# A down product with six of eleven row pairs in seven block products, and a copy moved ahead of rounding in one gate tile

## The chip, the cores and the metric

The kernel runs on 1 core of a Trainium2 chip. The metric is the device time of one execution in microseconds (us). Five engines work side by side and meet by semaphores: PE (TensorE, matmuls), DVE (VectorE), ACT (ScalarE), POOL (GpSimd) and SP (SyncE, which issues most DMAs). Each engine takes its instructions in the order of the program.

## The reference

One decoder layer over S = 512 positions of width D = 1024, in float32: a combined input projection, four retention heads, four attention heads over keys that an indexer selects, an output projection, a layer norm, and then a SwiGLU feed-forward of 2816 hidden columns with a last layer norm. Only the feed-forward's part matters here:

```python
FFN_HIDDEN = -(-(8 * D_MODEL) // (3 * 256)) * 256      # 2816
# x (512, 1024) after the first norm; wgu (1024, 2 x 2816), wd (2816, 1024)
gate, up = split(x @ wgu)
h = silu(gate) * up                                    # (512, 2816)
y = layer_norm(DEEPNORM_ALPHA * x + h @ wd, lfg, lfb)  # (512, 1024)
```

The layer norm takes mean and variance over the 1024 columns of a position, then gain `lfg` and bias `lfb`.

## The kernel before

**Precision.** Every product is made of three matmuls in a rounded float32 type (`mm3`, lines 94 to 96): high x high, high x low and low x high halves of the two operands. A helper `split` makes the halves: ACT casts to the high half (L86); the low half is either a subtraction on DVE (L91), or, where the engine is given as None, ACT copies the negated high source (L88, scale -1) and a DMA that POOL issues adds to it in place (L89, an accumulate).

**Staging.** The hidden width is cut into 22 tiles of 128 rows. The gate and up products run over 22 cycles `g_cycle(n)`, each of which already multiplies by blocks: sums of weight blocks (`g_sum`, on DVE) are split (`g_conv(n, kind)`, kinds A to D) and multiplied with sums of activation blocks, 128x256 a matmul (`g_mm`, L846); copies from PSUM (`t7` is the copy on L907, followed by the add on L916) and an order written out by hand tie the cycles together. In cycle n the splits of tile n+1 and n+2 are made. The results are the hidden activations `hu`, tiles [128 hidden, 512 positions], four to a buffer.

**Down product.** The 22 hidden tiles make 11 pairs. The output's 1024 columns are done in two halves of 512: first the left half for all pairs (banks `left`, in the profile `dl`), then the right (`right`, in the profile `dr`). For a pair m, `conv_w` splits 1024 weight columns a partition (`dh`, `dl` as weight tiles, from `draw`, a ring of three raw buffers that SP loads), `conv_h` splits the two hidden tiles once (`h`), and `d_mm` multiplies into the four position blocks b, two hidden tiles by three matmuls of 128x512 each. Weight halves lie in rings of four (`wh`, `wl`), so a cast for step i+4 waits for PE to leave step i. `take` adds a bank to the residual `y` (ALPHA y + bank), `stat` collects the norm's statistics. The last four pairs of the right half go block by block, so that each block's norm runs under the next block's matmuls; the last block's right half ends in a bank of its own (`dc`). The norm's gain and bias are loaded into `gf` (`gbf`) at the start of the stage.

The schedule is manual: each engine's order is the order of the code.

Of the kernel before, what the change touches and what calls it, by code (L numbers as in the profile page):

```python
# [15 lines left out]
P = 128  # L16
# [37 lines left out]
def hybrid_layer_kernel(ctx: ExitStack, tc: tile.TileContext, xT, x, pos, w0, wf, wt, wo,  # L54
# [12 lines left out]
    def psd(name):  # L67
        return psp.tile([P, 512], F32, tag="d", name=name)
# [987 lines left out]
    def d_load(j):
        c, g = divmod(j, 6)
        if c < 2:
            draw[j] = wp.tile([P, 4, S], F32, tag="raw", name=f"draw{j}")
            for k in range(2 * g, min(2 * g + 2, HC)):  # L1060
                i = 2 * (k % 2)
                dma(draw[j][:, i:i + 2], wd[k, :, :, c * S:c * S + S])

    def conv_w(i):
        if i >= 2 * HC:
            return
        c, m = divmod(i, HC)
        j = 6 * c + m // 2
        wh = wp.tile([P, 1024], F32R, tag="wh", bufs=4, name=f"dh{i}")
        wl = wp.tile([P, 1024], F32R, tag="wl", bufs=4, name=f"dl{i}")  # L1070
        src = draw[j][:, 2 * (m % 2):2 * (m % 2) + 2].rearrange("p k c -> p (k c)")
        split(V, wh, wl, src)
        dw[i] = wh, wl
        if m % 2 or m == HC - 1:
            d_load(j + 3)

    def conv_h(m):
        if m >= HC:
            return
# [12 lines left out]
        for k in range(2):  # L1092
            dh[2 * m + k] = hi[:, k * S:k * S + S], lo[:, k * S:k * S + S]

    def d_mm(acc, i, b, first, last, cs=slice(0, S)):
        wh, wl = dw[i]
        for k in range(2):
            h, l = dh[2 * (i % HC) + k]
            bs = slice(b * P, b * P + P)
            ws = slice(k * S + cs.start, k * S + cs.stop)  # L1100
            mm3(acc, h[:, bs], l[:, bs], wh[:, ws], wl[:, ws], first and k == 0, last and k == 1,
                **({} if cs.start == 0 and cs.stop == S else {"skip_group_check": True}))

    y = x1
    cl, cr = slice(0, S), slice(S, D)
# [49 lines left out]
    conv_w(2)  # L1155
    conv_h(2)
    for b in range(3):
        for i in range(2):
            d_mm(left[b], i, b, i == 0, False)
    conv_w(3)  # L1160
    conv_h(3)
    for i in range(2):
        d_mm(left[3], i, 3, i == 0, False)
    for i in range(2, HC):
        conv_w(i + 2)
        conv_h(i + 2)
        for b in range(NB):
            d_mm(left[b], i, b, False, i == HC - 1)

    right = [psd(f"dr{b}") for b in range(NB)]  # L1170
    for i in range(HC, 2 * HC - TAIL):
        conv_w(i + 2)
        if i - HC < NB:
            take(i - HC, cl, left[i - HC])
            stat(i - HC, 0, cl)
        for b in range(NB):
            d_mm(right[b], i, b, i == HC, b == NB - 1 and i == 2 * HC - TAIL - 1)
# [100 lines left out]
```

## Time and profile before

| | us |
|---|---|
| median of 3 runs (628.85 to 629.33) | 629.03 |
| the profiled execution's own time | 628.54 |
| its span in the profile | 626.8 |
| PE busy (3768 matmuls) | 617.3 |
| DVE busy | 478.2 |
| ACT busy | 299.6 |
| POOL busy | 95.4 |

The times of instructions in the trace count from the start of the span. The span is a little shorter than the execution's own time, which also holds what lies around it. An engine's busy time is the union of its instructions, without the issuing of DMAs; matmuls are pipelined, so that one lasts longer than the distance to the next. "x2" in a row of the timeline joins two instructions of one kind that follow each other. A releaser in brackets is what ended the idle time before an instruction.

### The profile page before, as it was taken

How to read it: one execution, taken by the hardware profiler on the slowest of the kernel's cores; microseconds unless marked ns; L12 is line 12 of the kernel's file. 1: busy time of each engine (PE TensorE's matmuls, PEld its weight loads, DVE VectorE, ACT ScalarE, POOL GpSimd, SP SyncE). 2: the span in 40 equal slices, each digit the busy share in tenths (PEclk: the TensorE clock that was granted, in tenths of full speed). 3: DMA queues.
4: the chain of work that ended last, by engine and by line, in shares of the span. 5: the costliest groups of instructions: out<-in, count | busy, mean ns of one | idle time of the engine just before them, and what ended most of it. 6: DMA issues, size and time to landing. Idle time of an engine off the chain costs nothing.

```text
span 626.8 us, 9712 instructions
## 1 busy us (share of the span) xinstructions
PE 617.3 (98%) x3768; PEld 551.8 (88%) x3768; DVE 478.2 (76%) x893; ACT 299.6 (48%) x529; POOL 95.4 (15%) x101
## 2 busy tenths in 40 slices
PE   9999999999999999999999999999999999999995
PEld 7988888888888778889999999999999988888884
DVE  6798687898879877899989898988889764333256
ACT  5644445335334656877555465555555653212200
POOL 1176322421463000332000000000000000000011
PEclk9999999999999999999999999999999999999999
DMA  9877344888534952894431323233231461422002
GB/s 316 280 225 222 108 122 110 213 170 196 136 104 138 339 217 68 207 179 102 151 135 68 135 73 131 84 119 115 89 135 68 151 220 67 135 90 79 0 35 100
DMA packets 25885, 88.24 MB, mean 141 GB/s; under 512 B 2752, under 2 KB 6144, under 8 KB 20208
## 3 DMA queue, kind: packets, MB, share of 16 engines
q1 hardware_dynamic: 18624, 71.51, 32.7%
q0 software_dynamic: 6480, 14.88, 12.7%
q10 hardware_dynamic: 736, 1.25, 0.6%
q8 instruction: 29, 0.48, 0.3%
q14 instruction: 16, 0.13, 0.1%
HBM read 69.80 MB, written 2.10 MB: 115 GB/s over the span
## 4 chain that ended last, share of the span: by engine, by line
PE 84%; DVE 9%; issue 3%; POOL 1%; ACT 1%; POOLq 0%; DVEq 0%; ACTq 0%
PE ga L846 17%; PE gc L846 9%; PE pf L95 5%; PE pf L94 5%; PE pf L96 5%; PE gb L846 4%; PE acc L205 4%; PE dl L94 3%; PE dl L96 3%; PE dl L95 3%; PE dr L96 3%; PE dr L94 3%; PE dr L95 3%; PE pt L94 2%; PE pt L96 2%
## 5 line engine op out<-in xcount | busy, mean ns | idle before, releaser
L91 DVE TENSOR_TENSOR dl<-draw,dh 128x1024 fp32r<-128x1024 f32 x22 | 26.9, 1225 | 59.0 <-ACT dh L86 59.0
L435 POOL TENSOR_TENSOR rs<-ve,half 128x1 f32<-128x1 f32 (+1 forms) x11 | 11.8, 1069 | 382.0 <-DVE ve L434 381.8
L86 ACT CAST wh<-raw 128x1024 fp32r<-128x1024 f32 x44 | 45.9, 1049 | 47.1 <-issue 19.8
L86 ACT CAST dh<-draw 128x1024 fp32r<-128x1024 f32 x22 | 23.1, 1049 | 68.1 <-PE dl L96 37.1
L94 PE MATMUL pf<-xh,wh 128*128 128x512 f32 x128 | 50.0, 391 | 0.0
L95 PE MATMUL pf<-xl,wh 128*128 128x512 f32 x128 | 50.0, 390 | 0.0
L96 PE MATMUL pf<-xh,wl 128*128 128x512 f32 x128 | 49.9, 390 | 0.0
L91 DVE TENSOR_TENSOR wl<-raw,wh 128x1024 fp32r<-128x1024 f32 x25 | 30.6, 1234 | 17.8 <-ACT wh L86 17.4
L94 PE MATMUL pt<-wh,xh 128*128 128x512 f32 x96 | 39.1, 408 | 0.0
L96 PE MATMUL pt<-wh,xl 128*128 128x512 f32 x96 | 37.5, 391 | 0.0
L95 PE MATMUL pt<-wl,xh 128*128 128x512 f32 x96 | 37.4, 390 | 0.0
L94 PE MATMUL dl<-dh,h 128*128 128x512 f32 x88 | 34.2, 389 | 0.0
L95 PE MATMUL dl<-dl,h 128*128 128x512 f32 x88 | 34.2, 389 | 0.0
L96 PE MATMUL dl<-dh,h 128*128 128x512 f32 x88 | 34.2, 389 | 0.0
L96 PE MATMUL dr<-dh,h 128*128 128x512 f32 (+1 forms) x88 | 33.4, 379 | 0.0
L95 PE MATMUL dr<-dl,h 128*128 128x512 f32 (+1 forms) x88 | 33.4, 379 | 0.0
L94 PE MATMUL dr<-dh,h 128*128 128x512 f32 (+1 forms) x88 | 33.4, 379 | 0.0
L815 DVE TENSOR_TENSOR gs<-graw,gs 128x512 f32<-128x512 f32 x44 | 30.3, 689 | 0.8
L815 DVE TENSOR_TENSOR gs<-graw 128x512 f32<-128x512 f32 x44 | 30.1, 685 | 0.0
L96 PEld LDWEIGHTS pf<-xh,wl 128*128 128x128 f32 x128 | 24.0, 188 | 5.2
L94 PEld LDWEIGHTS pf<-xh,wh 128*128 128x128 f32 x128 | 24.0, 188 | 4.6
L95 PEld LDWEIGHTS pf<-xl,wh 128*128 128x128 f32 x128 | 24.1, 188 | 4.6
(974 smaller groups left out, 1911.2 us busy)
## 6 DMA issues: line engine op xcount, KB each, us to landing
graw<-in_wgu_dram SPq DMA_DIRECT2D x22, 1024.0 KB, 4.8
draw<-in_wd_dram SPq DMA_DIRECT2D x22, 512.0 KB, 3.9
wl<-raw POOLq DMA_DIRECT2D x19, 512.0 KB, 5.8
raw<-in_wf_dram SPq DMA_DIRECT2D x8, 1024.0 KB, 6.7
raw<-in_wo_dram SPq DMA_DIRECT2D x8, 1024.0 KB, 4.9
raw<-in_wt_dram SPq DMA_DIRECT2D x6, 1024.0 KB, 5.1
w0s<-in_w_dram SPq DMA_DIRECT2D x8, 320.0 KB, 5.0
x<-in_x_dram SPq DMA_DIRECT2D x4, 512.0 KB, 5.7
```

What stands on the lines that cost most here:

```text
L86: A.copy(hi, src)
L91: eng_lo.tensor_tensor(lo, src, hi.bitcast(F32), op=ALU.subtract)
L94: T.matmul(acc, lhsT=lh, rhs=rh, start=first, stop=False, **kw)
L95: T.matmul(acc, lhsT=lh, rhs=rl, start=False, stop=False, **kw)
L96: T.matmul(acc, lhsT=ll, rhs=rh, start=False, stop=last, **kw)
L205: T.matmul(acc0[i][:, o:], lhsT=a[:, i * P:i * P + P], rhs=b[kt][:, o:], start=(kt == 0 and p == 0), stop=(kt == KT - 1 and p == 2))
L435: G.tensor_tensor(r[:, :n], e[:, :n], half[:, :n], op=ALU.pow)
L815: eng.tensor_tensor(t[dst], a, b, op=ALU.subtract)
L846: T.matmul(gp[n][acc], lhsT=a[:, i * S + k * P:i * S + k * P + P], rhs=parts[q][:, b, k], start=first and j == 0, stop=j == 11, skip_group ...
```

## The change

**Gate tile 2.** In the cycle of tile 2 the split of kind A for tile 3 stands behind the copy `t7` and its add, no longer ahead of them.

**Down product.** The pairs 0, 1, 2, 3 and 10 stay plain. The pairs 4 to 9 make three units (2, 3, 4) of two pairs. In a unit the positions are cut into two halves of 256, the hidden rows by pairs of tiles and the output columns into the left and right 512, and the 2x2 block product is made of seven products (q = 1 to 7) of sums of blocks in place of eight. Each product of a unit is one step: `w_prep(i)` splits its weights (step i+4 is prepared behind step i), `aprep` its activations, and `w_mm(i)` makes 12 matmuls of 128x512 into two banks. The order is q = 1, 5, 6, 2, 7, 4, 3, for each q the units 2, 3, 4. The banks X, Y and `left` gather products of several q and are added to `y` by `take` and by the new uses of `add_to`. New on DVE are the sums of blocks (s1 to s4 of activations, in the tiles `ts` and `t3s`; t1, t2, t4 of weights in the tiles `tw` or in place, t3 in place). Where `low` is None (the weights of q = 1, the activations of q = 1, 2, 7, 4, 3) the low halves go through POOL's accumulate: 3 of 512 KB and 15 of 256 KB; the down stage before had none. A sum or a product is named with its unit behind it: t1_2 is t1 of unit 2, p7_3 the split weights of q = 7 of unit 3, r1_4 the raw weights r1 of unit 4. Raw weights come as r1, r2a, r2b, r3a, r4, r5a, r5b through the same ring of three buffers. The gain and bias `gbf` are loaded in the middle of the stage (behind step 10), no longer at its start. The tail by blocks takes the plain pairs 0 to 3 and uses `add_to`.

```diff
         if n == 1:
             for m in range(FIRST):
                 g_silu1(m)
-        else:
+        if n not in (1, 2):
             g_conv(n + 1, "A")
...
         V.tensor_tensor(gp[n]["t7"], gp[n]["t7"], c, op=ALU.add)
+        if n == 2:
+            g_conv(3, "A")
...
+    PLAIN = [0, 1, 2, 3, 10]
+    UNITS = [2, 3, 4]
...
+    def wprep(key, pieces, low=V):
+        wh = wp.tile([P, 1024], F32R, tag="wh", bufs=4, name=f"dh{key}")
+        wl = wp.tile([P, 1024], F32R, tag="wl", bufs=4, name=f"dl{key}")
+        n = 1024 // len(pieces)
+        for i, src in enumerate(pieces):
+            hi, lo = (t[:, i * n:i * n + n] for t in (wh, wl))
+            if len(src.shape) == 3:
+                hi, lo = (t.rearrange("p (k c) -> p k c", c=S) for t in (hi, lo))
+            split(low, hi, lo, src)
+        dw[key] = wh, wl
...
+    def aprep(q, j, src, low):
+        i, half = divmod(slot_n[0], 2)
+        if half == 0:
+            slot_n[1] = big.tile([P, 2, 2, S], F32R, tag=slot_tags[i], name=f"slot{i}")
+        slot_n[0] += 1
+        t = slot_n[1][:, half]
+        split(low, pq(t[:, 0]), pq(t[:, 1]), src)
+        da[q, j] = t
...
+    def s1_(j):
+        ts[j] = tmp(f"ts{j}")
+        V.tensor_tensor(pq(ts[j]), blk(j, 1, 0), blk(j, 1, 1), op=ALU.add)
+
+    def s2_(j):
+        V.tensor_tensor(pq(ts[j]), pq(ts[j]), blk(j, 0, 0), op=ALU.subtract)
...
+    def t2_(j):
+        for q in range(2):
+            V.tensor_tensor(b22(j)[:, q], b22(j)[:, q], tw[j, q], op=ALU.subtract)
+
+    def t4_(j):
+        for q in range(2):
+            V.tensor_tensor(tw[j, q], b21(j)[:, q], b22(j)[:, q], op=ALU.subtract)
...
+    WORDER = [(q, j) for q in (1, 5, 6, 2, 7, 4, 3) for j in UNITS]
+
+    def w_prep(i):
+        q, j = WORDER[i]
+        prep[q](j)
...
+    def w_mm(i, banks, first):
+        q, j = WORDER[i]
+        wh, wl = dw[f"p{q}_{j}"]
+        a = da[q, j]
+        for n in range(2):
+            for t in range(2):
+                ss = slice(n * Q + t * P, n * Q + t * P + P)
+                ws = slice(n * S, n * S + S)
+                mm3(banks[t], a[:, 0, ss], a[:, 1, ss], wh[:, ws], wl[:, ws], first and j == UNITS[0] and n == 0,
+                    j == UNITS[-1] and n == 1, skip_group_check=True)
...
-    gf = big.tile([P, 2, D], F32, tag="s4", name="gbf")
-    for i, v in enumerate((lfg, lfb)):
-        dma(gf[:, i], row(v, D))
...
+    for j in UNITS:
+        s1_(j)
+    for j in UNITS:
+        aprep(1, j, blk(j, 0, 0), None)
+    conv_h(10)
+    t1_(2)
+    conv_w(0, 10)
+    r1_load(4)
+    w_prep(0)
+    r2a = raw_load("r2a", [(i, wd[4 + i, :, 1, S:]) for i in range(4)])
...
+    l_step(3)
+    for j in UNITS:
+        s2_(j)
+    for j in UNITS:
+        aprep(6, j, pq(ts[j]), V)
+    t2_(2)
+    w_prep(2)
+    r3a = raw_load("r3a", [(i, wd[4 + i, :, 1, :S]) for i in range(4)])
+    t2_(3)
+    t2_(4)
...
+    home_of = {1: X, 5: Y, 6: X, 2: left[:2], 7: X, 4: left[2:]}
+    gf = None
+    for i in range(18):
+        q, j = WORDER[i]
+        w_mm(i, home_of[q], q in (1, 5))
...
+        elif i == 7:
+            aprep(7, 2, pq(t3s[2]), None)
+            t3_(2)
+        elif i == 8:
+            for u in (3, 4):
+                aprep(7, u, pq(t3s[u]), None)
+        elif i == 9:
+            t3_(3)
+        elif i == 10:
+            t3_(4)
+            for u in UNITS:
+                aprep(4, u, blk(u, 1, 1), None)
+            gf = big.tile([P, 2, D], F32, tag="s8", name="gbf")
+            for k, v in enumerate((lfg, lfb)):
+                dma(gf[:, k], row(v, D))
+        elif i == 12:
+            for u in UNITS:
+                aprep(3, u, pq(ts[u]), None)
...
+        if i < 17:
+            w_prep(i + 4)
...
+        if i == 3:
+            r4_load(2)
+        elif i == 7:
+            r4_load(3)
+            r4_load(4)
+        elif i == 8:
+            r5a = raw_load("r5a", [(n, wd[4 + n, :, 1, S:]) for n in range(4)])
+        elif i == 9:
+            r5b = raw_load("r5b", [(n, wd[8 + n, :, 1, S:]) for n in range(2)] + [(2, wd[10, :, :, S:])])
+        elif i == 10:
+            d_load(1, 0)
+        elif i == 15:
+            d_load(1, 1)
...
+    for i in range(18, 21):
+        w_mm(i, [right[0], right[1]], True)
+        conv_w(1, last4[i - 18])
+    for b in (2, 3, 0, 1):
+        d_mm(right[b], 1, 10, b, b >= 2, True)
+    conv_w(1, last4[3])
```

On ACT in the cycle of gate tile 2 (`gt` are `t2` and `t7`, `ga` and `gc` banks of PSUM, `gh3A` the high half of the split of kind A for tile 3, `gs` its sums), the difference reads:

```order
 L86 CAST gh2D<-graw_2579 128x512
 L885 COPY gt_2985<-ga_2692 128x256
+L907 COPY gt_2985<-ga_2692 128x256
 L86 CAST gh3A<-gs_1_2946 128x512
 L86 CAST gh3A<-gs_0_2945 128x512
-L907 COPY gt_2985<-ga_2692 128x256
 L86 CAST gh4B<-graw_2857 128x512 x2
```

The copy has moved ahead of the two casts; on DVE the add that reads it has moved ahead of gl3A's two subtractions in the same way.

On ACT in the first part of the down stage (`draw` and `r` are raw weights, `hu` the hidden activations), the order before was:

```order
-L86 CAST dh_5506<-draw_5401 128x1024
-L86 CAST h_1_5510<-hu_3109 128x1024
-L86 CAST dh_5550<-draw_5401 128x1024
-L86 CAST h_1_5510<-hu_3109 128x1024
-L86 CAST dh_5571<-draw_5492 128x1024
-L86 CAST h_2_5575<-hu_3630 128x1024
```

and what stands some way behind the same first four rows now (`slot` holds split activations, `ts` their sums, `dhp_4_...` and `dlp_4_...` the halves of p1_4, the weights of q = 1 of unit 4; `r_4_5595` is r1_4):

```order
+L86 CAST dhp_3_5643<-r_3_5550 128x1024
+L88 ACTIVATE dlp_3_5644<-r_3_5550 128x1024
+L86 CAST slot_5684<-ts_5567 128x512
+L86 CAST slot_5684<-ts_5569 128x512
+L86 CAST slot_5689<-ts_5571 128x512
+L86 CAST dhp_4_5694<-r_4_5595 128x1024
+L88 ACTIVATE dlp_4_5695<-r_4_5595 128x1024
```

Casts of weights and of activations took turns one pair at a time; now the weights of q = 1 of unit 4 stand behind the three casts of the sums for q = 6, and their low half is a copy on ACT that an accumulate of POOL follows.

On ACT in the middle of the block steps (`dhp_2_5938`, `dhp_3_5962` and `dhp_4_5996` are the weights of q = 7 for units 2, 3 and 4, from r4; `slot<-hu` are activations of q = 4):

```order
+L86 CAST dhp_2_5938<-r_2_5832 128x1024
+L86 CAST dhp_3_5962<-r_3_5913 128x1024
+L86 CAST slot_5934<-hu_3630 128x512
+L88 ACTIVATE slot_5934<-hu_3630 128x512
+L86 CAST slot_5986<-hu_4151 128x512
+L88 ACTIVATE slot_5986<-hu_4151 128x512
+L86 CAST slot_5986<-hu_4672 128x512
+L88 ACTIVATE slot_5986<-hu_4672 128x512
+L86 CAST dhp_4_5996<-r_4_5916 128x1024
```

Where before one cast of 1024 weight columns followed another, six operations of 512 columns now stand between the weights of units 3 and 4. On SP the loads that feed this place, with what follows them, are now (`r_2_5832`, `r_3_5913` and `r_4_5916` are r4 of units 2, 3 and 4):

```order
+L80 DMA r2b<-in_wd_dram 128x512 x4
+L80 DMA r3a<-in_wd_dram 128x512 x4
+L80 DMA r_2_5832<-in_wd_dram 128x2x512 x2
+L80 DMA r_3_5913<-in_wd_dram 128x2x512 x2
+L80 DMA r_4_5916<-in_wd_dram 128x2x512 x2
+L80 DMA r5a<-in_wd_dram 128x512 x4
+L80 DMA r5b<-in_wd_dram 128x512 x2
+L80 DMA r5b<-in_wd_dram 128x2x512
 L80 DMA gbf<-in_lfg_dram 128x1024
 L80 DMA gbf<-in_lfb_dram 128x1024
```

The two loads of `gbf`, which stood behind the first loads of the stage, now come behind these and ahead of the raw weights of the tail.

## Rows read from the trace of the kernel before

**Rows 1.** The page, part 1: busy time, share of the span, instructions of each engine.

```profile
PE 617.3 (98%) x3768; PEld 551.8 (88%) x3768; DVE 478.2 (76%) x893; ACT 299.6 (48%) x529; POOL 95.4 (15%) x101
```

**Rows 2.** Waits of PE: waiting line, releaser, us in total, times, longest us.

```profile
PE ga L846 <- ACT gt L907: 0.5, 1, 0.5
PE gc L846 <- DVE gt L916: 0.2, 1, 0.2
```

**Rows 3.** Windows, left and right half: length; PE, PEld, DVE, ACT, POOL; clock, DMA, GB/s.

```profile
498.90:558.90 60.00, 60.00 (x268) 49.74 (x267) 28.40 (x28) 22.73 (x24) 0.00 (x0) 1.00 0.39 132
558.90:616.00 57.10, 57.10 (x264) 47.72 (x263) 24.67 (x33) 8.40 (x8) 3.45 (x3) 1.00 0.14 47
```

**Rows 4.** Tile `dl`: duration ns least/median/most, first and last start us, forms.

```profile
L94 PE MATMUL dl<-dh,h x88: 389/389/396, 499.1 to 558.3; 128*128 128x512 f32 x88
```

**Rows 5.** Timeline around gate tile 2: start us, us, instruction, [idle before it <-releaser].

```profile
305.65 1.14 ACT L86 CAST gh3A<-gs 128x512 fp32r<-128x512 f32 x2 [2.36 <-DVE gs L815]
306.69 0.36 ACT L907 COPY gt<-ga 128x256 f32<-128x256 f32 x1
...
307.11 0.38 PE L846 MATMUL ga<-part,gh2C 128*128 128x256 f32 x1 [0.49 <-ACT gt L907]
...
307.29 1.29 DVE L91 TENSOR_TENSOR gl3A<-gs,gh3A 128x512 fp32r<-128x512 f32 x2
308.49 0.42 DVE L916 TENSOR_TENSOR gt<-gt,gc 128x256 f32<-128x256 f32 x1
...
308.96 0.39 PE L846 MATMUL gc<-parts,gh2D 128*128 128x256 f32 x1 [0.16 <-DVE gt L916]
...
313.69 1.29 DVE L91 TENSOR_TENSOR gl3C<-gs,gh3C 128x512 fp32r<-128x512 f32 x2
...
314.94 0.28 PE L846 MATMUL ga<-parts,gl3C 128*128 128x256 f32 x1
```

**Rows 6.** Groups by line: instruction xcount | busy us, mean ns | idle before.

```profile
L815 DVE TENSOR_TENSOR gs<-graw 128x512 f32<-128x512 f32 x44 | 30.1, 685 | 0.0
L88 ACT ACTIVATE wl<-raw 128x1024 fp32r<-128x1024 f32 x19 | 20.1, 1056 | 0.0
```

**Rows 7.** Timeline of ACT and DVE at the start of the down stage.

```profile
502.08 1.05 ACT L86 CAST h<-hu 128x1024 fp32r<-128x1024 f32 x1
503.03 1.05 ACT L86 CAST dh<-draw 128x1024 fp32r<-128x1024 f32 x1
...
503.36 1.22 DVE L91 TENSOR_TENSOR h<-hu,h 128x1024 fp32r<-128x1024 f32 x1
504.49 1.22 DVE L91 TENSOR_TENSOR dl<-draw,dh 128x1024 fp32r<-128x1024 f32 x1
```

**Rows 8.** DMA issues of the whole run: xcount, KB each, median us to landing.

```profile
graw<-in_wgu_dram SPq DMA_DIRECT2D x22, 1024.0 KB, 4.8
...
wl<-raw POOLq DMA_DIRECT2D x19, 512.0 KB, 5.8
...
g0A<-gs POOLq DMA_DIRECT2D x2, 256.0 KB, 5.1
...
gbf<-in_lfb_dram SPq DMA_DIRECT2D x1, 512.0 KB, 7.4
```

**Rows 9.** Tile `draw`: its loads' issues (ns) and landings (us), least/median/most.

```profile
L80 SPq DMA_DIRECT2D draw<-in_wd_dram x22: 539/577/1208, 475.8 to 572.4; - x22
...
DMA to landing us min/median/max: 3.5/3.9/5.8
```

**Rows 10.** Line 89, all accumulates: POOL's issues (ns) and the landings (us).

```profile
L89 POOL DMA_DIRECT2D wl<-raw x19: 869/884/949, 31.1 to 185.8; - x19
...
DMA to landing us min/median/max: 3.3/5.3/9.5
```

**Rows 11.** Tile `wl`: landings of its accumulates of 512 KB.

```profile
DMA to landing us min/median/max: 4.5/5.8/9.5
```

**Rows 12.** Window over the stretch with most accumulates, columns as in rows 3.

```profile
30.00:190.00 160.00, 160.00 (x782) 135.04 (x782) 131.87 (x277) 66.20 (x90) 67.70 (x68) 1.00 0.63 161
```

More of the change, by code (lines that the diff above doesn't have):

```diff
@@ L1050, in hybrid_layer_kernel @@
     HC = NF // 2
-    TAIL = 4
-    draw, dw, dh = {}, {}, {}
-    STORE = (("s3", "s5"), ("s0", "s7"), ("X0", "X1"), ("s1", "s6"), ("s8", "s2"), ("s10",))
+    PLAIN = [0, 1, 2, 3, 10]
+    UNITS = [2, 3, 4]
+    dw, dh, da = {}, {}, {}
+    STORE = {0: ("s3", "s5"), 1: ("s0", "s7"), 5: ("X0",)}
     halves = {}
[L1056 to L1075, printed above, removed]
+    def raw_load(name, pieces):
+        t = wp.tile([P, 4, S], F32, tag="raw", name=name)
+        for i, src in pieces:
+            n = src.shape[1] // S if len(src.shape) == 2 else src.shape[1]
+            dma(t[:, i:i + n].rearrange("p k c -> p (k c)") if len(src.shape) == 2 else t[:, i:i + n], src)
+        return t
@@ L1077, in conv_h, with d_load, conv_w @@
+    draw = {}
+    def d_load(c, g):
+        pairs = ((0, 1), (2, 3), (10,))[g]
+        draw[c, g] = raw_load(f"draw{c}_{g}", [(2 * i, wd[k, :, :, c * S:c * S + S]) for i, k in enumerate(pairs)])
+    def conv_w(c, k):
+        if k == 10:
+            t, i = draw[c, 2] if c == 0 else r5b, 0 if c == 0 else 2
+        else:
+            t, i = draw[c, k // 2], 2 * (k % 2)
+        wprep((c, k), [t[:, i:i + 2].rearrange("p k c -> p (k c)")])
     def conv_h(m):
-        if m >= HC:
-            return
@@ L1092, in conv_h, with d_mm @@
         for k in range(2):
-            dh[2 * m + k] = hi[:, k * S:k * S + S], lo[:, k * S:k * S + S]
-    def d_mm(acc, i, b, first, last, cs=slice(0, S)):
-        wh, wl = dw[i]
+            dh[m, k] = hi[:, k * S:k * S + S], lo[:, k * S:k * S + S]
+    def d_mm(acc, c, m, b, first, last, cs=slice(0, S)):
+        wh, wl = dw[c, m]
         for k in range(2):
-            h, l = dh[2 * (i % HC) + k]
+            h, l = dh[m, k]
             bs = slice(b * P, b * P + P)
             ws = slice(k * S + cs.start, k * S + cs.stop)
-            mm3(acc, h[:, bs], l[:, bs], wh[:, ws], wl[:, ws], first and k == 0, last and k == 1,
-                **({} if cs.start == 0 and cs.stop == S else {"skip_group_check": True}))
+            mm3(acc, h[:, bs], l[:, bs], wh[:, ws], wl[:, ws], first and k == 0, last and k == 1, skip_group_check=True)
@@ new lines, in b22, with b21, t3_ @@
+    def b22(j):
+        return r2a[:, 2 * (j - 2):2 * (j - 2) + 2] if j < 4 else r2b[:, :2]
+    def b21(j):
+        return r3a[:, 2 * (j - 2):2 * (j - 2) + 2] if j < 4 else r2b[:, 2:]
+    def t2_(j):
+        for q in range(2):
+            V.tensor_tensor(b22(j)[:, q], b22(j)[:, q], tw[j, q], op=ALU.subtract)
+    def t4_(j):
+        for q in range(2):
+            V.tensor_tensor(tw[j, q], b21(j)[:, q], b22(j)[:, q], op=ALU.subtract)
+    def t3_(j):
+        v = r4[j].rearrange("p (q k) c -> p q k c", k=2)
+        V.tensor_tensor(v[:, :, 0], v[:, :, 1], v[:, :, 0], op=ALU.subtract)
@@ L1158, in hybrid_layer_kernel @@
         for i in range(2):
-            d_mm(left[b], i, b, i == 0, False)
-    conv_w(3)
+            d_mm(left[b], 0, i, b, i == 0, False)
+    conv_w(0, 3)
+    r1_load(3)
     conv_h(3)
     for i in range(2):
[L1163 to L1166, printed above, removed]
-        for b in range(NB):
[L1168 to L1177, printed above, removed]
@@ L1178, in hybrid_layer_kernel, with l_step @@
-    for i in range(2 * HC - TAIL + 2, 2 * HC):
-        conv_w(i)
-    last4 = range(2 * HC - TAIL, 2 * HC)
+        d_mm(left[3], 0, i, 3, i == 0, False)
+    for j in UNITS:
[8 more added lines that the diff above has]
+    r2a = raw_load("r2a", [(i, wd[4 + i, :, 1, S:]) for i in range(4)])
+    def l_step(k):
+        for b in range(NB):
+            d_mm(left[b], 0, k, b, False, False)
@@ new lines, in hybrid_layer_kernel @@
+    l_step(2)
+    t1_(3)
+    for j in UNITS:
+        aprep(5, j, pq(ts[j]), V)
+    w_prep(1)
+    r2b = raw_load("r2b", [(i, wd[8 + i, :, 1, S:]) for i in range(2)] + [(2 + i, wd[8 + i, :, 1, :S]) for i in range(2)])
+    t1_(4)
+    l_step(3)
+    for j in UNITS:
+        s2_(j)
+    for j in UNITS:
+        aprep(6, j, pq(ts[j]), V)
[4 more added lines that the diff above has]
+    t2_(4)
+    l_step(10)
+    for j in UNITS:
+        s3_(j)
@@ new lines, in hybrid_layer_kernel @@
+    w_prep(3)
+    X = [psd(f"dx{t}") for t in range(2)]
+    Y = [psd(f"dy{t}") for t in range(2)]
+    home_of = {1: X, 5: Y, 6: X, 2: left[:2], 7: X, 4: left[2:]}
[3 more added lines that the diff above has]
+        w_mm(i, home_of[q], q in (1, 5))
+        if i == 0:
+            for u in UNITS:
+                s4_(u)
+        elif i == 1:
+            t4_(2)
+            t4_(3)
+        elif i == 2:
+            for t in range(2):
+                take(t, cl, X[t])
+        elif i == 3:
+            aprep(2, 2, blk(2, 0, 1), None)
+            aprep(2, 3, blk(3, 0, 1), None)
+        elif i == 4:
+            aprep(2, 4, blk(4, 0, 1), None)
+        elif i == 6:
+            t4_(4)
+        elif i == 7:
[14 more added lines that the diff above has]
+        elif i == 12:
+            for u in UNITS:
+                aprep(3, u, pq(ts[u]), None)
+        if i < 17:
+            w_prep(i + 4)
+        else:
+            conv_w(1, 10)
+        if i == 3:
[11 more added lines that the diff above has]
+            d_load(1, 1)
+        if i == 5:
+            for t in range(2):
+                take(t, cr, Y[t])
+            for t in range(2):
+                take(2 + t, cr, Y[t])
+        elif i == 8:
+            for t in range(2):
+                add_to(t, cr, X[t])
+        elif i == 14:
+            for t in range(2):
+                take(2 + t, cl, X[t])
+            for t in range(2):
+                add_to(2 + t, cr, X[t])
+        elif i == 16:
+            for b in range(2):
+                add_to(b, cl, left[b])
+                stat(b, 0, cl)
+        elif i == 17:
+            for b in range(2, NB):
+                add_to(b, cl, left[b])
+                stat(b, 0, cl)
@@ L1182, in hybrid_layer_kernel @@
+    right = {b: psd(f"dr{b}") for b in (2, 3, 0, 1)}
+    last4 = PLAIN[:4]
+    for i in range(18, 21):
[4 more added lines that the diff above has]
+    conv_w(1, last4[3])
     for b in range(NB - 1):
         for i in last4:
-            d_mm(right[b], i, b, False, i == last4[-1])
-        take(b, cr, right[b])
+            d_mm(right[b], 1, i, b, False, i == last4[-1])
+        add_to(b, cr, right[b])
@@ L1197, in hybrid_layer_kernel @@
     for i in last4:
-        d_mm(right[b][:, :Q], i, b, False, i == last4[-1], slice(0, Q))
-    take(b, cr, right[b])
+        d_mm(right[b][:, :Q], 1, i, b, False, i == last4[-1], slice(0, Q))
+    add_to(b, cr, right[b])
     stat(b, 1, slice(S, S + Q))
```

48 lines of the change are left out of this document (41 added, 7 removed).

## The prediction

> **What bounds the kernel now.** I read four views in turn. The page's busy times put PE at 617.3 of 626.8 us, 98% [rows 1]: DVE has 24% of the span free, ACT 52%, POOL 85%. PE's own waits then show only two short ones outside the warm-up, 0.5 and 0.2 us, both in the third gate tile, n = 2 [rows 2]. The windows of the down product's two halves say the same for the stage that changes: PE busy 60.00 of 60.00 us and 57.10 of 57.10, at granted clock 1.00, with DVE at 28.40 and 24.67, ACT at 22.73 and 8.40, and DMA shares of 0.39 and 0.14 [rows 3]. The other engines wait for PE there or for each other. So the time is the number of PE rows, and fewer rows shorten it unless a feeder comes late. The pace of a row: the 88 first matmuls of `dl` start from 499.1 to 558.3, one of three, so 261 rows lie between: 59.2/261 = 0.2268 us a row [rows 4] (389 ns each, overlapping).
>
> **Fewer matmuls.** Before, 22 hidden rows x 2 halves x 4 blocks x 3 = 528 matmuls of 512 columns. After, five plain pairs need 5 x 2 x 8 x 3 = 240 and 21 block steps 12 each, 252: 492 in all. 36 x 0.2268 = **-8.17 us**. With no wait, matmul n starts at 499.14 + 0.2268n and block step i at n = 120 + 12i, so at 526.36 + 2.72i.
>
> **Gate tile.** Before, ACT runs two casts (1.14 from 305.65) ahead of the copy at 306.69, and PE waits 0.49 for it; DVE runs gl3A (1.29 from 307.29) ahead of the add, and PE waits 0.16 [rows 5]. The move takes both waits away, 0.65. What is late next: DVE has no gap from 302 to 318, so gl3C, which starts at 313.69, keeps its time. Its first half ends about 314.4 (half of 1.29 on), and PE, which used it at 314.94, now wants it at 314.29. With some 0.05 for the release I take 0.15 back: **-0.50**; bounds -0.65 (DVE itself gains, if the reordered add lets it run ahead) and -0.3 (gl3C late by as much again).
>
> **What is added.** Sums on DVE: 30 of 512 columns at 685 ns, pitch 0.60 in a row, and 3 of 1024 [rows 6] (1.14); six activation lows of 0.6 and 12 more takes and adds to banks at 0.6: 18 + 3.4 + 3.6 + 7.2 = 32 us; the count of 1024-wide lows stays at 33. DVE: 53 + 32 = 85 of 109 us, 78%. ACT: 21 casts and 15 copies of 512 at 0.52 (the pair of rows 5 takes 1.14), three more casts, three copies at 1.06 [rows 6]: +25, 56 of 109. Neither is the bound by its sum, so the cost lies in lateness alone. A 1024 split in a row costs ACT 0.95 and DVE 1.14 (502.08 to 503.03; 503.36 to 504.49) [rows 7].
>
> DMA: 18 POOL accumulates where there were none. A 1 MB load lands in 4.8 [rows 8], one of 512 KB in 3.5 at best [rows 9]: 2.2 + 1.3 per 512 KB. SP's issues follow 0.6 apart (577 ns) [rows 9]. An accumulate's issue takes POOL 0.87 to 0.95; landings of all sizes run 3.3/5.3/9.5 (least, median, most) [rows 10], those of 512 KB 4.5/5.8/9.5 [rows 11], the median at 256 KB is 5.1 [rows 8]. With 3.3 as the best at 256 KB an accumulate is 2.1 + 1.2 per 256 KB. How loads and accumulates share the engines no row tells for this stage: I let each transfer queue behind those issued before it, whoever issues; the other bound is that none waits for another.
>
> I walked the new order with these prices. Most steps keep 1 to 3 us of slack. Three places don't.
>
> *A, p1_4's low half (step 2, wanted at 532.0).* ACT's four casts of 1024 end at 504.9 (three at 0.95 from 502.08), the six operations for q=1 at 508.1 (0.52 each), the cast of h's pair 10 at 509.0; DVE then takes its low (1.14), t1_2 (2 x 0.6) and the low of weight pair 10 (1.22 in all), to 512.8 with the releases between them. That frees the third raw buffer. r1_4's two loads go out at 512.9 and 513.4, land about 519.4 and 520.8 behind p1_2's accumulate (2.4). Then on DVE t1_4 and three s2 (to 523.2), on ACT the last cast of activations, p1_4's cast at 523.9 and copy to 525.9, POOL's issue at 526.2; at 5.8 it lands at 532.0. I take **0**; an accumulate landing in 9.5 makes it +3.7.
>
> *B, p7_3 and p7_4 (steps 13 and 14, lows wanted at 561.95 and 564.65).* PE's step 5 frees a weight buffer at 542.9; then DVE, in order: p2_2's low from 543.96 (1.14), four takes (2.4), t4_4 (1.2), p2_3's low, t3_2, p2_4's low: 552.2. That frees r2b, and SP issues r4_3 and, 1.2 later, r4_4. Ahead of them on the DMA engines stand two accumulates (256 KB, issued 550.7 and 551.7, served by 555.2). r4_3 lands at 558.6, not 557.2; t3_3 to 559.9, cast to 560.95, low to 562.2: 0.3 late. Then ACT's order has the three activation splits of q=4 (6 x 0.52 = 3.1) before p7_4's cast, which so ends at 565.05, its low at 566.3: 1.3 more. **+1.6**. If loads pass accumulates it is 0.15; if those accumulates land in 9.5, 5.3.
>
> *C, the splits of q=3 (steps 18 to 20, wanted from 577.0 with B's wait in it).* Issued 567.4 to 569.5 behind gbf, whose two loads took up to 7.4 before [rows 8], and draw(1,0): 2 MB, 5.2. They land between 577 and 581.4, 0.2 to 1 us in hand. **0**, bounds 0 and 3.7.
>
> The gbf load itself is not wanted before the last LN; SP's later loads behind it are the tail weights, wanted after 580. The tail and its LN are row for row the old ones.
>
> A page of the Trainium skill speaks against accumulates beside a busy DVE. The rows: while POOL issued accumulates between 30 and 190 us, DVE was busy 131.87 of 160.00 [rows 12], and the 19 issues stayed at 869 to 949 ns [rows 10]. By the Trainium skill, SBUF — State Buffer, section "Who interferes with whom", a VectorE instruction with two SBUF inputs holds off a GpSimd instruction that reads SBUF until it is done; the trace doesn't bear that out for these issues. By that rule each issue would wait up to one DVE operation, and the sum would be about 1.2 more.
>
> **Sum.** The profiled execution's 628.54 - 8.17 - 0.50 + 1.6 = 621.5; the median of the runs is 629.03, 0.49 above it: **622.0 us**.
>
> **Rivals.**
> 1. *No wait at all.* The accumulates land nearer their best (3.3, 4.5) and the loads are not held: 620.4, 620.2 if the gate tile gives its whole 0.65. For it: DMA shares of 0.39 and 0.14 before. Against: B has two causes, and ACT's order alone leaves 0.15.
> 2. *Several places late.* A, C and B together, 3 to 7.5 us, or a DVE that runs 1 us behind my walk at each take: 623.4 to 628. For it: three places have under 1 us in hand, and DVE runs in order at 78%: one late load holds all that is queued behind its sum. Against: the waits don't add in full, since a PE that waits once gives the later ones the same time back.
> 3. *POOL's issues held off by DVE.* As a mechanism here: the issue before A's landing starts while DVE runs t2's sums (0.6 to 1.2 long), so A comes up to 1.2 late and the time is 623.2. For it: DVE is to run 78% busy there. Against: no stretched issue with DVE busy 82% of a stretch [rows 10, 12].
> 4. *Slower than before.* Every accumulate of this stage lands like the longest, 9.5, being queued behind 1 MB loads throughout: A +3.7, B +5.3, C +3.7, 12.7 us, which gives 633.1. It decides from 8.67 us of waits: 3x + 1.6 = 8.67, x = 2.4, a mean landing of 8.2. Against: the median at 512 KB is 5.8 [rows 11] in a stretch with DMA share 0.63 [rows 12], and the new stage stays below that.
> 5. *The change doesn't do what it says*: PE's clock falls in new waits, or the bank order makes PE wait for takes. Banks have three steps, 8.2 us, between last use and next, and the granted clock is 1.00 in both halves [rows 3]. Below 2%, in with 2.
>
> **Numbers.** Forecast (0.3 to 3 us of waits, 620.9 to 623.3): 0.50. No wait: 0.20. Several places: 0.20. Held-off issues: 0.05. Slower or level: 0.05. The range goes from rival 1's 620.2 to 625.5, which leaves out the upper half of rival 2 and rival 4, under 0.2. 0.2% of 629.03, about what a measurement tells from no change, is 1.26 us: faster means under 627.8. Faster 0.93, same 0.03, slower 0.04.
>
> **What the profile after would show.** PE with 36 rows fewer at the same 0.2268; in the third gate tile no wait on the copy, and a wait of some 0.15 on gl3C. PE's waits in the down stage: 0.3 and 1.3 on lows of `p7` steps behind r4_3's loads and the q=4 casts; none on p1_4 (right if its accumulate lands by 532.0) or on the slots of q=3. POOL issues at 0.87 to 0.95. I am wrong if accumulates land over 7 us, if DVE is late at a place I count as free (t4, p5_4, p6_2), or if r4 loads pass the accumulates.

## The result, and the profile after

The changed kernel takes 625.04 us (median of 5 runs, 623.99 to 627.01) against 629.12 (628.85 to 629.33): a ratio of 0.9942, interval 0.992 to 0.9963. It is faster, and inside the range of 620.2 to 625.5, but 3 us above the 622.0 forecast, inside the rival "several places late" (623.4 to 628). The runs of one kernel now spread over 3 us where those of before spread over 0.5 (over 1.4 to 1.8 in the larger sets beside the experiments); that is a second thing to explain. The profiled execution's own time is 625.04, its span 623.2.

The busy times of the page, which answer to [rows 1], and the waits of PE, which answer to [rows 2] (waiting line, releaser, us in total, times, longest):

```profile
PE 609.9 (98%) x3732; PEld 544.4 (87%) x3732; DVE 511.5 (82%) x950; ACT 325.2 (52%) x577; POOL 115.7 (19%) x119
```

```profile
PE dx L95 <- DMA dlp<-r: 2.9, 1, 2.9
PE warm L188 <- DVE cold L185: 1.2, 1, 1.2
PE dx L95 <- DVE dlp L91: 0.6, 1, 0.6
PE ga L846 <- DVE gl3C L91: 0.5, 1, 0.5
PE pf L96 <- DVE wl L91: 0.3, 1, 0.3
```

36 matmuls are gone (3768 to 3732). The two waits of the third gate tile have turned into one at gl3C. Two new waits stand in the block steps (`dx` is the bank pair X), both on low halves of weights: one on an accumulate, one on DVE. Where they lie, in PE's timeline:

```profile
532.46 0.39 PE L94 MATMUL dx<-dhp,slot 128*128 128x512 f32 x1
535.74 0.50 PE L95 MATMUL dx<-dlp,slot 128*128 128x512 f32 x1 [2.89 <-DMA dlp<-r]
```

```profile
569.29 0.50 PE dx L95
```

The first is step 2, p1_4: the matmul begins 3.28 behind the one ahead of it, 3.05 more than the pitch of 0.23. The second (a line of the chain of waits) is step 14, p7_4, with 0.78 more than the pitch. About 0.11 follows each of them. The chain of waits of the stage names what ended last ahead of them (start, us, what):

```profile
513.76 8.76 DMA r<-in_wd_dram
522.52 0.02 issue
...
527.95 7.74 DMA dlp<-r
...
557.24 7.71 DMA r<-in_wd_dram
564.95 0.51 ACT slot L86
...
566.94 1.06 ACT dhp L86
568.01 1.24 DVE dlp L91
```

The first two are r1_4's second load (8.8 us) and p1_4's accumulate (7.7), both ahead of the first wait (place A of the prediction). The third is r4_4's second load, with q = 4's splits on ACT behind it, ahead of the second wait (place B). The chain leaves the last at 564.95 for ACT; it landed at 565.5, 8.2 from its issue. All three took 2 to 5 us longer than the median of their kind had [rows 8, 9, 11]. The table of DMA issues, which answers to [rows 8]:

```profile
r<-in_wd_dram SPq DMA_DIRECT2D x12, 512.0 KB, 5.9
...
slot<-hu POOLq DMA_DIRECT2D x9, 256.0 KB, 7.2
...
dlp<-r POOLq DMA_DIRECT2D x3, 512.0 KB, 7.7
...
slot<-ts POOLq DMA_DIRECT2D x3, 256.0 KB, 9.7
...
gbf<-in_lfb_dram SPq DMA_DIRECT2D x1, 512.0 KB, 9.8
```

How full the DMA engines are is read from the window over the stage: in the kernel before, and then in the changed one (columns as in [rows 3]; DMA share and GB/s are the last two).

```profile
499.00:616.00 117.00, 117.00 (x529) 97.37 (x528) 52.97 (x61) 31.13 (x32) 3.45 (x3) 1.00 0.27 90
```

```profile
499.00:609.00 110.00, 106.49 (x472) 87.72 (x472) 83.29 (x113) 56.81 (x81) 22.73 (x20) 1.00 0.72 189
```

The share went from 0.27 to 0.72. The mean over the stage hides how full the engines were ahead of the two waits. In the changed kernel (a packet counts whole where it starts, so that a short window can pass 1):

```profile
513.00:523.00 10.00, 10.00 (x46) 8.29 (x45) 4.51 (x8) 3.47 (x5) 2.38 (x2) 1.00 1.14 246
554.00:569.00 15.00, 14.67 (x65) 11.83 (x63) 9.71 (x10) 8.52 (x15) 5.35 (x5) 1.00 0.97 293
```

Of the rise of the mean the accumulates' part is read from part 3 of the two pages (queue q0 carries what POOL issues: packets, MB, share of 16 engines); before, then after:

```profile
q0 software_dynamic: 6480, 14.88, 12.7%
```

```profile
q0 software_dynamic: 10608, 20.39, 17.9%
```

17.9% of 623.2 less 12.7% of 626.8 is 32 us of all 16 engines, 0.29 of a stage of 110 us, for 5.5 MB: 5.8 us a MB. The loads of q1 carried 71.51 MB in 32.7% of 626.8, 2.9 us a MB. A byte accumulated held the engines twice as long as a byte loaded. That is not only a matter of the crowd: in the kernel before, a window that holds one accumulate of 0.52 MB and no other transfer has a share of 0.61 over 4.53 us, 5.3 us a MB.

```profile
104.39:108.92 4.53, 4.53 (x22) 3.75 (x21) 2.88 (x7) 2.02 (x4) 2.21 (x2) 1.00 0.61 116
```

**The account.** With no wait the sum was 628.54 - 8.17 - 0.50 = 619.87. The waits add 3.16 and 0.89: 623.92. The rest of 1.1 is older than the change: PE stood 1.06 behind the kernel before already when it came to the third gate tile, after small waits in the first 200 us, whose code is the same. In later profiles of variants with this same code it was anything from 0 to 1.1.

### The profile page after: what moved, and what is told of

Same layout as the page of the kernel before. It is cut to its first block, busy times and chain, and to the rows that moved or that the text cites. A ratio compares the mean times of both kernels' runs of the same rounds, so it can differ in the third digit from the quotient of the medians.

```text
span 623.2 us, 9845 instructions
## 1 busy us (share of the span) xinstructions
PE 609.9 (98%) x3732; PEld 544.4 (87%) x3732; DVE 511.5 (82%) x950; ACT 325.2 (52%) x577; POOL 115.7 (19%) x119
## 3 DMA queue, kind: packets, MB, share of 16 engines
q0 software_dynamic: 10608, 20.39, 17.9%
## 4 chain that ended last, share of the span: by engine, by line
PE 70%; DVE 15%; DMA 6%; ACT 3%; issue 3%; POOL 1%; SPq 0%; POOLq 0%; ACTq 0%; DVEq 0%
PE ga L846 17%; PE gc L846 9%; PE pf L96 5%; PE pf L95 5%; PE pf L94 5%; PE gb L846 4%; DMA r<-in_wd_dram 3%; PE pt L94 3%; PE pt L96 3%; PE pt L95 3%; DVE gs L815 2%; PE mx L96 2%; PE mx L94 2%; PE mx L95 2%; PE dr L94 2%
## 5 line engine op out<-in xcount | busy, mean ns | idle before, releaser
L89 POOL DMA_DIRECT2D slot<-hu x9 | 10.9, 1317 | 230.1 <-ACT slot L88 229.5
L397 DVE MAX8 m<-score 128x8 f32<-128x256 f32 (+2 forms) x48 | 26.8, 558 | 1.1
L89 POOL DMA_DIRECT2D wl<-raw x19 | 16.9, 890 | 57.1 <-ACT wl L88 50.3
L398 DVE MATCH_REPLACE8 score<-m,score 128x256 f32<-128x256 f32 (+2 forms) x48 | 26.0, 542 | 0.0
L380 ACT ACTIVATE lg<-lg 128x256 f32<-128x256 f32 (+2 forms) x24 | 10.9, 474 | 24.6 <-PE lg L379 22.4
L96 PEld LDWEIGHTS pt<-wh,xl 128*128 128x128 f32 x96 | 18.0, 188 | 3.9
L95 PEld LDWEIGHTS pt<-wl,xh 128*128 128x128 f32 x96 | 18.1, 189 | 3.1
L94 PEld LDWEIGHTS pt<-wh,xh 128*128 128x128 f32 x96 | 18.1, 189 | 3.1
```

The costliest lines, as they stand in the source:

```text
L380: A.activation(lp[:, :n], lp[:, :n], AF.Relu)
L397: V.max(m8, a)
L398: V.match_replace(out=a, in_to_replace=m8, in_values=a, imm_value=TAKEN)
```

## The experiments

Twelve kernels ran, each beside the kernel before on the same chip (its median was 629.10 to 629.19). "Ratio" is to those runs, with its 95% interval.

**The changed kernel again, and the clock.** No edit.

> The changed kernel itself once more, for the spread of its runs and for its waits in a second profile. Theory (transfers): the wait at p1_4's low half is made of loads and accumulates that queue on the DMA engines, so it comes back with 2 to 3.5 us, the one at p7_4's low half with 0.5 to 1.5, and the median is 625 +- 1. Rival (chance): the 2.9 us wait belonged to one execution; the second profile shows under 1 us there and a median near 622.

626.43 (623.10 to 627.99), ratio 0.9947, 0.9929 to 0.9965. The waits came back at the same places: 2.9 and 0.8. The profiled execution was the slowest of the six, at 627.99, and its timeline shows what the first profile didn't:

```profile
531.39 0.39 PE L94 MATMUL dx<-dhp,slot 128*128 128x512 f32 x1
534.72 0.79 PE L95 MATMUL dx<-dlp,slot 128*128 128x512 f32 x1 [2.93 <-DMA dlp<-r]
535.31 0.63 PE L96 MATMUL dx<-dhp,slot 128*128 128x512 f32 x1
535.73 0.63 PE L94 MATMUL dx<-dhp,slot 128*128 128x512 f32 x1
...
540.85 0.45 PE L94 MATMUL dy<-dhp,slot 128*128 128x512 f32 x1
541.14 0.39 PE L95 MATMUL dy<-dlp,slot 128*128 128x512 f32 x1
```

Behind the wait matmuls start 0.427 apart, not 0.227, from 535.3 to 540.9. The window over that stretch gives the granted clock in its third figure from the end: 0.50, the lower level of 1.2 GHz; the same window of the first profile has 1.00.

```profile
535.50:541.00 5.50, 5.50 (x15) 4.24 (x14) 4.52 (x8) 1.14 (x2) 0.00 (x0) 0.50 0.58 191
```

```profile
535.50:541.00 5.50, 5.26 (x23) 4.38 (x24) 3.19 (x5) 2.39 (x4) 0.00 (x0) 1.00 0.55 188
```

14 rows from 535.31 to 541.14 took 5.83 in place of 3.18, and 0.36 more lay ahead of them: 3.0 us, as much as the wait itself. It came in this execution and not in the first one profiled, and so is a source of the spread; how much of it is taken up in the last section. I had expected the wait to come back and not this.

**The gate edit alone**, in the kernel before.

```diff
-        else:
+        if n not in (1, 2):
             g_conv(n + 1, "A")
...
+        if n == 2:
+            g_conv(3, "A")
```

> The kernel before with the edit of gate tile 2 alone. Theory: PE's waits of 0.5 and 0.2 us go and gl3C's low half costs 0.1 to 0.2, so the time falls by 0.4 to 0.55, to about 628.6. Rival (DVE sets the pace there): all of it comes back at gl3C, a wait of 0.65, and the time stays at 629.1.

628.54, ratio 0.9991, 0.9982 to 0.9999. The interval just excludes no change, and the size fits. PE's timeline has one wait there:

```profile
315.24 0.39 PE L846 MATMUL ga<-parts,gl3C 128*128 128x256 f32 x1 [0.49 <-DVE gl3C L91]
```

By the starts of the same matmuls in the two traces, PE gained 1.16 up to the add and gave 0.75 back at gl3C: 0.41 net, as in the changed kernel. Both are larger than forecast (0.65 and 0.15): idle time counts from the end of the matmul ahead, which in an unbroken row lies 0.16 behind the next start, and the start behind the one that waited came 0.10 late as well, so each wait costs 0.26 more than its idle time. The net is not larger.

**p1_4's low half on DVE.**

```diff
-        1: lambda j: wprep(f"p1_{j}", [odd(r1[j], 0)], None),
+        1: lambda j: wprep(f"p1_{j}", [odd(r1[j], 0)], V if j == 4 else None),
```

> The changed kernel with p1_4's low half subtracted on DVE, in place of the copy on ACT and POOL's accumulate. Theory: the wait at p1_4 (2.9 us) was the landing of that accumulate and goes, since DVE has the half by 529 against 532.5; the waits at p7_3 and p7_4 then come out as forecast, up to 1.6 together, since PE is no longer late there: 622 to 622.7. Rival (DVE): 1.14 us more on DVE's queue make p5_2's low half late by 0.2 to 1.2 and the rest with it: 623 to 624. Rival (not this half): the time stays at 625.

624.36 (623.29 to 624.84), ratio 0.9921, 0.9908 to 0.9934. In the waits of PE the one at p1_4 is gone; two at p7 stand, each costing 1.03 by the starts:

```profile
PE dx L95 <- DVE dlp L91: 1.5, 2, 0.8
```

By the window from 562 to 568, where both lie, the granted clock was 1.00. So A's accumulate was the first wait, and B, with PE on time, costs 2.1 and more with its small steps, against 1.6 forecast; the median is 1.7 above the 622 to 622.7 expected.

**The splits of q = 4 behind p7_4's**, the order on which B's larger half was forecast to hang.

```diff
         elif i == 10:
             t3_(4)
-            for u in UNITS:
-                aprep(4, u, blk(u, 1, 1), None)
...
             w_prep(i + 4)
+            if i == 10:
+                for u in UNITS:
+                    aprep(4, u, blk(u, 1, 1), None)
```

> The changed kernel with the three activation splits of q = 4 moved behind p7_4's weight split on ACT. Theory as forecast: these 3.1 us on ACT hold p7_4's cast, and the second wait (0.8 us at p7_4's low half) goes: 624.2. Rival (load): r4 of unit 4 lands so late that t3_4 and so the cast could not be earlier by more than 0.2 us: no change, 625.0, and the wait stays with DVE's t3_4 as what ended ACT's idle time.

627.90 (624.86 to 630.78), ratio 0.9981, 0.9965 to 0.9997: worse than the changed kernel. In ACT's timeline the cast for p7_4 was released by t3_4, and so by r4_4's load, no longer by ACT's order:

```profile
567.54 1.05 ACT L86 CAST dhp<-r 128x1024 fp32r<-128x1024 f32 x1 [3.42 <-DVE r L1173]
```

PE still waited 0.20 there, then 0.60 on an accumulate of q = 4 that now came late, and 0.23 behind it. The load was as late as the order; moving the order alone moved the wait. The profile doesn't show why the median is worse: with the 2.7 at p1_4 its waits add up to 3.7 us, as in the second profile of the changed kernel, and the clock fell behind the first in both. Runs at a mean clock of 0.997 to 0.998 took 624.86 to 627.88, those at 0.991 up to 630.78.

**Half of r2b's loads taken out of the way of p1_4's accumulate.**

```diff
-    r2b = raw_load("r2b", [(i, wd[8 + i, :, 1, S:]) for i in range(2)] + [(2 + i, wd[8 + i, :, 1, :S]) for i in range(2)])
+    r2b = raw_load("r2b", [(i, wd[8 + i, :, 1, S:]) for i in range(2)])
...
     r3a = raw_load("r3a", [(i, wd[4 + i, :, 1, :S]) for i in range(4)])
+    for i in range(2):
+        dma(r2b[:, 2 + i], wd[8 + i, :, 1, :S])
```

> The changed kernel with r2b's second half (512 KB) loaded behind r3a, so that 512 KB in place of 1 MB of r2b's loads lie ahead of p1_4's accumulate on the DMA engines. Theory (transfers queue): its landing falls from 7.7 us to about 6.4, PE's wait there from 3.1 to under 1.9; with the shorter wait the granted clock stays at 1.00 behind it, and the median comes to 623 to 624. Rival (an accumulate of these strides is slow by itself): the landing stays at 7.5 or more, the wait at 3, and the median at 625 to 626.5.

623.17 (622.36 to 624.27), ratio 0.9905, 0.9892 to 0.9918. The table of DMA issues for the moment of its issue, 527.68, has p1_4's accumulate landing in 5.0 us, and the waits of PE have 0.7 on it:

```profile
dlp<-r POOLq DMA_DIRECT2D x1, 512.0 KB, 5.0
```

```profile
PE dx L95 <- DMA dlp<-r: 0.7, 1, 0.7
```

That is 2.7 less for 512 KB less of loads, twice what I had counted, and the clock was 0.997 in all four runs. The theory that transfers hold each other up stands, and the rival, an accumulate that is slow by itself, falls.

**The activation splits of q = 1 on DVE.**

```diff
-        aprep(1, j, blk(j, 0, 0), None)
+        aprep(1, j, blk(j, 0, 0), V)
```

> The changed kernel with the three activation splits of q = 1 subtracted on DVE, so that three accumulates of 256 KB less lie ahead of r1_4's loads. Theory (transfers queue): r1_4's second load, which took 8.8 us from its issue to its landing, takes 6 to 7.5; but DVE's 1.8 us more put its issue up to 1.3 later, so PE's wait at p1_4 falls by 0 to 1.5 only. Rival (the accumulates aren't in its way): the load still takes 8.5 or more, and the wait grows by about 1.

629.58 (627.52 to 630.97), ratio 1.0007, 0.9998 to 1.0016: the whole gain lost. r1_4's second load took 8.3 in place of 8.8, out of the forecast 6 to 7.5, and went out 1.2 later; PE's wait at p1_4 grew to 3.6, with the clock at the lower level behind it:

```profile
PE dx L95 <- DMA dlp<-r: 3.6, 1, 3.6
```

The three accumulates of 256 KB were not what slowed that load most.

**No accumulate at all in the down stage**: None replaced by V in all nine places of `wprep` and `aprep`.

> The changed kernel with every low half of the down stage subtracted on DVE, no accumulate left in it. Theory: loads alone land within 6 us and the wait at p1_4 goes, but DVE's work grows by 15 x 0.6 + 3 x 1.14 = 12.4 us to some 101 of 113, and its order makes other halves late: waits of 1 to 4 us in all, each under 2, clock at 1.00: 622 to 625. Rival (accumulates cost nothing but what DVE would): waits over 5 us, slower than 626.

621.46 (620.85 to 621.70), ratio 0.9876, 0.9862 to 0.9890: 3.6 us less than the changed kernel in its first set, better than expected. One wait is left in the stage, at p7_4, 0.48 by the starts. r1_4's second load lands in 5.7, r4_4's in 5.7.

**p1_4 on DVE, r3a loaded ahead of r2b, t2_4 behind t4_3, the splits of q = 4 ahead of p7_3's cast.** The last of its edits:

```diff
         elif i == 9:
             t3_(3)
+            for u in UNITS:
+                aprep(4, u, blk(u, 1, 1), None)
```

> Both late places mended: p1_4's low half on DVE; r3a loaded ahead of r2b, so that r4 of unit 3 takes the raw buffer that p2_3 frees, one step earlier, and r4 of unit 4 isn't queued behind it; the splits of q = 4 ahead of p7_3's cast on ACT; t2_4 behind t4_3. Theory (place B is the chain of raw buffers and ACT's order): no wait over 0.3 at p7_3 or p7_4, all 36 matmuls come out: 620.6 to 621.5. Rival (another place takes over, the q = 4 or q = 3 accumulates at steps 15 to 20): a wait of 0.5 to 2 there, 621.5 to 623.

625.60 (623.93 to 628.01), ratio 0.9946, 0.9929 to 0.9962: slower than with p1_4's edit alone. Neither theory had this. The swap of loads changed nothing: r4_3's load goes out at 551.09, and at 550.95 without it; its buffer was already the one that p2_3 frees, and my walk had that wrong. The splits put three accumulates among r4_4's loads, and the second of these, issued at 553.95, took 11.6 us by the table of DMA issues for that moment:

```profile
r<-in_wd_dram SPq DMA_DIRECT2D x1, 512.0 KB, 11.6
```

against 9.5 in the kernel with p1_4's edit alone. PE waited 0.8 us for p7_3's low half, 2.3 for p7_4's cast and 0.8 for its low half, and the clock fell behind the last.

**No accumulate, and q = 4's splits behind p7_4's**, as in the fourth experiment but on DVE.

> The kernel without accumulates in the down stage, with the three splits of q = 4 moved behind p7_4's weight split on ACT and DVE. Theory: the one wait left in its stage, 0.5 us at p7_4's low half, is DVE's three lows of q = 4 (1.8 us) ahead of that half, and goes: 0.5 to 0.6 less than without the move, 620.9. Rival: DVE at 89% gives it back at the next halves: 621.4.

620.22 (619.95 to 620.34), ratio 0.9855, 0.9841 to 0.9868. By its waits PE stands nowhere in the down stage, and the window over the stage has it busy throughout:

```profile
PE warm L188 <- DVE cold L185: 1.2, 1, 1.2
PE ga L846 <- DVE gl3C L91: 0.5, 1, 0.5
```

```profile
499.00:609.00 110.00, 110.00 (x503) 91.64 (x502) 97.53 (x136) 46.11 (x62) 4.50 (x3) 1.00 0.45 144
```

Its own profiled time is 619.95 against the 619.87 of the account without waits: the 36 matmuls come out whole, with DVE busy 89% of the stage and the DMA share at 0.45. The runs spread over 0.4 us.

**The same, with kind C's split ahead of the sums in gate tile 2.**

```diff
-        if n > 1:
+        if n > 2:
             g_sum(n + 2)
         g_conv(n + 1, "C")
+        if n == 2:
+            g_sum(4)
```

> The same, and in gate tile 2 the split of kind C for tile 3 ahead of the four sums for tile 4 on DVE. Theory: PE's wait of 0.5 us at gl3C's low half, which the gate edit left behind, goes too: 620.4. Rival: the sums come late by 1.2 us instead and the wait moves to the split of kind A for tile 4: no gain.

620.00, ratio 0.9853, 0.9839 to 0.9866: the wait at gl3C is gone and one of 0.2 at the next cycle's add has come. The difference to the kernel above, 0.2, lies within the intervals; this doesn't decide.

**Weights of q = 1 on DVE, the 15 activation accumulates kept; and the reverse, the three weight accumulates alone.**

```diff
-        1: lambda j: wprep(f"p1_{j}", [odd(r1[j], 0)], None),
+        1: lambda j: wprep(f"p1_{j}", [odd(r1[j], 0)], V),
```

> The changed kernel with all three weights of q = 1 subtracted on DVE and the 15 accumulates of activations kept. Theory (the engines' load): the wait at p1_4 goes, those at p7_3 and p7_4 stay with 1 to 1.3 us each, since accumulates of 256 KB still stand among r4's loads; the clock stays at 1.00: 623 to 624.5. Rival (the weights' accumulates are the whole cost): as without any accumulate, 621.5.

> The kernel without accumulates but for the three of q = 1's weights (512 KB each). Theory (the engines' load): with the 15 others gone r1_4 lands sooner, so the wait at p1_4 falls from 3.1 to between 0 and 1.5 us and nothing else waits over 0.6: 621.5 to 623, clock at 1.00. Rival (an accumulate is slow whatever else runs): the wait stays at 2.5 or more and the clock falls behind it in part of the runs: 624 to 627.

The first: 623.39, ratio 0.9905, 0.9890 to 0.9920, waits at p7 and one of 0.9 on an accumulate of q = 4, the clock at 0.997 or more. The second: 627.05, ratio 0.9960, 0.9947 to 0.9972. There the theory missed, and the rival's signs came, with a time just above its 624 to 627: PE waits 4.8 us at p1_4, and the window behind the wait has the clock at 0.50.

```profile
PE dx L95 <- DMA dlp<-r: 4.8, 1, 4.8
```

```profile
537.00:542.00 5.00, 5.00 (x13) 3.85 (x13) 2.34 (x5) 0.13 (x1) 0.00 (x0) 0.50 0.64 210
```

Set side by side, the landing of three transfers tells the two places apart (us from issue to landing, of each single DMA):

| kernel | r1_4, second load | p1_4's accumulate | r4_4, second load |
|---|---|---|---|
| changed | 8.8 | 7.7 | 8.2 |
| three weight accumulates alone | 8.6 | 8.6 | 5.4 |
| 15 activation accumulates alone | 6.7 | - | 10.1 |
| none | 5.7 | - | 5.7 |

The loads of r1_4 and r4_4 in the second and third of these kernels, by the table of DMA issues for the moments of their issue (514.04 and 560.70; 513.12 and 552.81):

```profile
r<-in_wd_dram SPq DMA_DIRECT2D x1, 512.0 KB, 8.6
r<-in_wd_dram SPq DMA_DIRECT2D x1, 512.0 KB, 5.4
...
r<-in_wd_dram SPq DMA_DIRECT2D x1, 512.0 KB, 6.7
r<-in_wd_dram SPq DMA_DIRECT2D x1, 512.0 KB, 10.1
```

Place A's load is slowed in the main by the weights' accumulates, place B's by the activations'. No activation accumulate is needed for A's wait: p1_2's and p1_3's accumulates and r2b's loads were enough, which is why the theory of the last experiment missed. Its rival's reason, an accumulate that is slow whatever else runs, doesn't hold: p1_4's landed in 5.0 with fewer loads beside it. That the wait came out longer, 4.8, because DVE's work on the activations lies ahead of it is likely and not shown.

## Why the prediction was right, and by how much it missed

The number came out inside the range, 0.5 from its upper end, and that is in part luck: the wait at place A was in no term of the sum, and the second set of the same kernel, 626.43, lies outside.

- **Fewer matmuls, -8.17: right.** The kernel without accumulates ends at 619.95, 0.08 from the account without waits.
- **Gate tile, -0.50: right in size** (-0.41 by the starts), with both its terms too small by about the same (1.16 gained and 0.75 given back, against 0.65 and 0.15).
- **Place A: the step that failed.** I put p1_4's accumulate at the old median of 5.8 us [rows 11] and r1_4's second load at 7.4, and took 0. They measured 7.7 and 8.8; the wait was 3.16 with what follows it, near the +3.7 that the prediction gives as the bound. The error is one: the price of a transfer was the median of a mixture, and the rule was that each queues "behind those issued before". The runs show that later ones count too: r4_4's second load took 9.5 with two accumulates just ahead of it and r5a behind, 11.6 with three more accumulates behind, 5.7 with r5a and no accumulate. The trace of before had it already. Behind the median of [rows 11], 8 of the 19 accumulates met no load and landed in 4.5 to 5.6; the one issued at 132.07, with a 1 MB load 0.08 behind it, took 9.2:

```profile
raw<-in_wt_dram SPq DMA_DIRECT2D x1, 1024.0 KB, 6.7
wl<-raw POOLq DMA_DIRECT2D x1, 512.0 KB, 9.2
```

The prediction named accumulates over 7 us as a sign of being wrong, and 12 of the 18 took longer than that. It also held that the stage stays below a DMA share of 0.63; it came to 0.72.

- **Place B: right in place and kind, mis-sized.** Forecast 0.3 and 1.3; 1.03 and 1.03 with PE on time, 0.89 in all in the changed kernel, where PE came 3.2 late. That a wait gives later ones their time back, as the second rival said, isn't borne out as a rule: in the repeated profile PE came 6.1 late, r4_4's second load took 9.6 in place of 8.2, and the wait at p7_4 cost 1.03 again. Of its two causes I priced the order on ACT as the larger; the load was as late (t3_4 ends within 0.2 us of ACT's splits). The walk also had r4_3's load wait for r2b's buffer; it took the one that p2_3 frees.
- **Place C: right**, no wait on the slots of q = 3 in the changed kernel, though their accumulates took 9.7 in the median.
- **POOL's issues held off by DVE: no sign.** The accumulates of unbroken 2 KB rows (`slot<-ts`, `slot<-t3s`) were issued in 856 to 906 ns, as [rows 10], and those of two pieces a partition in 1185 to 1552, while DVE was busy three quarters of the stage. Whether the issue of a DMA is an instruction of the kind that the cited rule speaks of, no run shows.
- **The spread and the clock were in no step.** I had put a fall of the clock under 2%.
- **Slower than before** needed 8.67 us of waits. One variant came level (1.0007), with a wait of 3.6, the lower clock behind it and 2.6 us of later waits: closer than the 0.05 that I gave, by a way that I had not priced.

By the Trainium skill, DMA: Bandwidth & Descriptors, section "Issuing engines are not separate DMA queues", transfers issued by different engines run on the same 16 DMA engines and interleave. The traces agree: the second loads of r1_4 and r4_4, issued by SP, took 5.4 to 5.7 us with no accumulate of POOL's among them and 6.7 to 11.6 with them.

## What to carry to other kernels

An accumulate by DMA takes work off DVE, but here each byte held the DMA engines twice as long as a load. Before 18 of them are put into a stage, count the engines' time (32 us here, on a share that went from 0.27 to 0.72), read the share at the place and not over the stage (1.14 and 0.97 ahead of the two waits), and look at which loads are issued within some 8 us to either side, about as long as these transfers took to land. DVE at 89% with an order that fits beat DVE at 76% with accumulates by 5 to 6 us. And when a wait of several microseconds is forecast for PE, price the granted clock behind it as well: in the repeated profile it doubled the wait.

## What the runs showed of the hardware that I had not expected

The granted clock fell to 0.50 for 3.4 to 6.8 us at or behind PE's waits of 2.7, 2.9, 3.6 and 4.8 us at p1_4, and behind 2.3 and 0.8 close together at p7_4; it stayed at 1.00 behind another 2.9 at p1_4, in the first profile, and behind two of about 0.8 at p7. What decides between the two waits of 2.9 no run here tells. That the fall is the whole of the spread between runs is not shown either: only profiled executions have a timeline, and the runs' mean clocks, 0.992 to 0.998 in the repeated changed kernel, go with their times but not strictly (626.08 at 0.997). In the kernel with q = 4's splits behind p7_4's, 627.81 stands at 0.998.
